# Ends of attention per 128 tokens with one inverse root on VectorE, earlier first gates and spread conditioning in a two-layer PEER block

## The chip, the cores and the metric

The kernel runs on one core of a Trainium2 chip. The metric is the device time of one execution in microseconds (us). The runs of the kernel before took 2294.64, 2292.17 and 2294.27 us, a median of 2294.27. One more execution was taken under the hardware profiler; every row below comes from it.

## The reference

A sequence of 256 tokens, 1024 wide, passes two layers and then two recurrent mixers (an LRU and a gated delta net) that are conditioned on a vector. One layer is, cut to what matters here:

```python
xn = rmsnorm(x, norm_mix[l])
u_pool, u_conv, u_diff, u_sc, u_mem = split(xn @ w_in[l])      # 256, 512, 768, 768, 256 columns
y_diff = diff_attention(u_diff)        # per head: softmax(q1 k1) - lam * softmax(q2 k2), times v
#   o = rmsnorm(o, subln_g) * (1 - lam_init)   per token and head (64 columns)
y_mem = memory_attention(u_mem, mem)   # softmax(q k) v over 256 memory rows, 4 heads
cat = stack([y_pool, y_conv, y_diff, y_sc, y_mem])             # groups 0 to 4, 256 columns each
cat = rmsnorm(cat, group_norm[l])      # per token and group
x = x + cat @ w_out[l]                 # 1280 x 1024
x = x + peer_ffn(rmsnorm(x, norm_ffn[l]))
```

The PEER part picks 16 of 16384 experts for each of 8 heads and token, with gates g. The kernel computes it densely: act = gelu(xn @ u.T) for all 16384 experts, times a gate matrix that is zero nearly everywhere, and that times v.

## The kernel before

All matrix products are in fp32 by three products of split operands: a tile from memory (`raw`) gives a high part `wh` (ScalarE, line 293) and a low part `wl` (VectorE, line 296), and TensorE adds high by high, high by low and low by high. TensorE is in use nearly throughout, so what counts is where it waits.

The program is a row of stages: mix0, peer0, mix1, peer1, lru, gdn, final. In the profiled execution mix0 ends at about 174 us, the u pass of peer0 runs to 630 and its v pass to 987, mix1 lasts to 1157, the u pass of peer1 to 1613 and its v pass to 1984.

**Mixing** (`mixing`, line 1033). The product with `w_in` runs in pieces; between its matmuls `tick` (here `fill`) advances background generators by a credit, and the order in which they are advanced is the order of the instructions on every engine. The generators are: a convolution (group 1), two lanes of differential attention (`diff_lane`, four units of two heads and 128 tokens each) and their end (`diff_end`), two lanes of memory attention (`mem_lane`) with `mem_end`, the short convolution (group 3) and the pooling (group 0). They take PSUM banks from a count (`bank`, `banks`, `free`) limited to `BANKS = 5`, and to `WBANKS = 4` once `wide`, the product with `w_out`, begins, since its four accumulators take the other four. `wide` takes the groups in the order `ZORDER = (3, 1, 0, 4, 2)` and calls `tick` until the next group is in the set `ready`: 8 matmuls of 128x512 per group, part and pair, 120 in all.

A group's norm needs an inverse root. `rsq` (lines 569 to 588) computes it by an integer guess and three Newton steps in 13 small instructions on GpSimd (POOL), after one VectorE instruction (line 577). Groups 0, 1 and 3 use it on sums over channels (`fT0`, `fT1`, `fT3`; their result goes through TensorE as a diagonal matrix). `diff_end` waits for all four units, squares (line 968), sums per head (972), calls `rsq` (`dsr`), scales (975 to 979), and goes to `finish_tok` (720), which squares again, calls `rsq` again (`ft2`), scales (728), transposes to channel layout on TensorE (`ident,do`) and hands the result to `into_z` (706), which writes the split parts `zTh` and `zTl`. `mem_end` has the one `rsq` of `finish_tok` (`ft4`; `mo` is its tensor).

**PEER** (`experts`, line 1215, and `v_pass`, 1365). The u pass has 64 steps of two expert tiles. Every few matmuls `tick` advances the scoring, the `routing` and then `scatter`, which builds the gates of the first 128 tokens as one-hot products: `hots` (lines 1275 and 1276, VectorE), `sums` (TensorE, `o,o`), `into` (1292 and 1294, evacuation into `big`). The gates of the other 128 tokens lie in memory and come back by `dense_load` (`gate<-dense`), to be multiplied in by `part` (line 1363). After the 64 steps the u pass runs whatever is left of routing and scatter, multiplies in the first two gate tiles, and splits the first tile of the v pass into `lasth` and `lastl`. The v pass then takes 128 tiles; in layer 1 it also advances, once per tile, the conditioning of the recurrent mixers (`adas`: products with `ada_w_2` on VectorE into `adacc`, lines 1448 and 1450, and a sum over partitions on TensorE, `adacc,ones`).

DMAs from memory to on-chip tiles are issued by SyncE (SP) in program order; an issue that must wait for a free buffer holds those behind it. `raw` has three buffers.

Of the kernel before, what the change touches and what calls it, by code (L numbers as in the profile page):

```python
# [86 lines left out]
class K:  # L87
# [617 lines left out]

    def into_z(self, l, g, ps):

        gc = self.col("group_norm", l)[:, 2 * g:2 * g + 2]
        i = yield from self.slot(g)
        zh, zl = [t[:, i:i + 2, :] for t in self.zT]  # L710
        for j in range(2):
            self.nc.scalar.activation(zh[:, j, :], ps[:, j, :], AF.Copy, scale=gc[:, j:j + 1])
        yield
        for j in range(2):
            self.nc.vector.scalar_tensor_tensor(zl[:, j, :], ps[:, j, :], gc[:, j:j + 1], zh[:, j, :],
                                                op0=OP.mult, op1=OP.subtract)
        self.ready.add(g)
        yield 0.8

    def finish_tok(self, l, g, y):  # L720
        ss = self.sm.tile([128, 2], F32, name=f"ftq{g}")
        junk = self.wk.tile([128, 2, 256], F32, name=f"fsq{g}", bufs=1)
        for c in range(2):
            self.nc.scalar.activation(junk[:, c, :], y[:, c, :], AF.Square, accum_out=ss[:, c:c + 1])
        yield
        rs = yield from self.rsq(ss, 256, [128, 2], f"ft{g}")
        for c in range(2):
            self.nc.vector.tensor_scalar(y[:, c, :], y[:, c, :], rs[:, c:c + 1], None, op0=OP.mult)
        yield 0.5
        ps = yield from self.bank()  # L730
        p = ps.rearrange("p (j t) -> p j t", j=2)
        for j in range(2):
            for c in range(2):
                self.tr(p[:, j, c * 128:(c + 1) * 128], y[:, c, j * 128:(j + 1) * 128])
        yield
        yield from self.into_z(l, g, p)
        self.free()
# [160 lines left out]
    def attend(self, ps, a, v, h0, o, lane):  # L898

        n = a.shape[1]  # L900
        for h in range(n):
            for k in range(2):
                i = 2 * (h % 2) + k
                self.tr(ps[h // 2][:, i * 128:(i + 1) * 128], a[:, h, k * 128:(k + 1) * 128])
            if h % 2:
                yield
        yield
        aT = self.wk.tile([128, n, 2, 128], F32, name="aT" + lane, bufs=1)
        for m in range(n // 2):
# [12 lines left out]

    def diff_lane(self, units, lane, V):
# [5 lines left out]
        for c, h0 in units:  # L929
# [11 lines left out]
            for i in range(2):  # L941
                nc.vector.scalar_tensor_tensor(s[:, i], pv[i], scale,
                                               V["alibi"][:, c, h0 + i, None, :].to_broadcast([128, 2, T]),
                                               op0=OP.mult, op1=OP.add)
                yield 0.7
                nc.vector.tensor_reduce(t[:, i, 0:2], s[:, i], axis=AX.X, op=OP.max, negate=True)
                yield 0.6
                for j in range(2):
                    nc.scalar.activation(s[:, i, j, :], s[:, i, j, :], AF.Exp, bias=t[:, i, j:j + 1],
                                         accum_out=t[:, i, 2 + j:3 + j])  # L950
            yield
            for i in range(2):
# [5 lines left out]
                yield 0.8  # L958
            yield from self.attend(ps, s[:, :, 0, :], V["v"], h0, V["o"][:, c, :], lane)
            V["n"] += 2  # L960

    def diff_end(self, l, V):
        nc = self.nc
        while V["n"] < 8:
            yield
        sq = self.wk.tile([128, 2, 256], F32, name="fsq2", bufs=1)
        o = V["o"]
        nc.scalar.activation(sq, o, AF.Square)
        yield
        yield  # L970
        ss = self.sm.tile([128, 8], F32, name="dss")
        nc.vector.tensor_reduce(ss, sq.rearrange("p c (h d) -> p (c h) d", d=64), axis=AX.X, op=OP.add)
        yield 0.6
        rs = yield from self.rsq(ss, 64, [128, 8], "dsr")
        nc.vector.tensor_scalar(rs, rs, 1.0 - (0.8 - 0.6 * math.exp(-0.3 * l)), None, op0=OP.mult)
        ov = o.rearrange("p c (h d) -> p (c h) d", d=64)
        nc.vector.tensor_mul(ov, ov, rs[:, :, None].to_broadcast([128, 8, 64]))
        yield 0.6
        nc.vector.tensor_mul(ov, ov, V["sub"][:, None, :].to_broadcast([128, 8, 64]))
        yield 0.6  # L980
        yield from self.finish_tok(l, 2, o)

    def mem_lane(self, units, lane, V):
# [5 lines left out]
        for c in units:  # L989
# [22 lines left out]
            V["n"] += 4  # L1012

    def mem_end(self, l, V):
        nc = self.nc
        while V["n"] < 8:
            yield
        r = self.sm.tile([128, 8], F32, name="mr")
        nc.vector.reciprocal(r, V["sum"])
        yv = V["o"].rearrange("p c (h d) -> p (c h) d", d=64)  # L1020
        nc.vector.tensor_mul(yv, yv, r[:, :, None].to_broadcast([128, 8, 64]))
        yield 0.7
        yield from self.finish_tok(l, 4, V["o"])
# [13 lines left out]
    def mixing(self, l):  # L1037
# [11 lines left out]
        M, V = {"n": 0}, {"n": 0, "alibi": alibi}  # L1049
# [29 lines left out]
        with self.ordered(*MPIN):  # L1079
# [12 lines left out]
            self.spawn(self.diff_end(l, V))  # L1092
# [6 lines left out]
            self.spawn(self.mem_end(l, M))  # L1099
# [5 lines left out]
            self.spawn(self.pool_mixer(l, self.kept(self.gemm_tok(xT, w, 18), "pu"), bd, poolm))  # L1105
            self.limit = WBANKS
# [107 lines left out]
    def experts(self, l, xT, big, skT, sc0, sc1):  # L1214
# [142 lines left out]
        self.split(big[:, 0, :], *[t[:, 0, :] for t in self.last])  # L1357
# [7 lines left out]
    def v_pass(self, l, big):  # L1365
# [23 lines left out]
        for e in range(128):  # L1389
# [771 lines left out]
RAW = 3  # L2161
VPIN = ("DVE", "Activation", "Pool", "PE")
# [131 lines left out]
```

## Time and profile before

| what | value |
|---|---|
| median of three runs | 2294.27 us (2292.17 to 2294.64) |
| the profiled execution, and its span | 2297.74 us, 2296.0 us |
| mean granted clock of TensorE over the span | 0.979 |
| TensorE (PE) busy | 2204.5 us, 96% |
| VectorE (DVE), ScalarE (ACT), GpSimd (POOL) busy | 1768.8, 1225.2 and 651.3 us |

The profiled execution took 1.74 us more than its span and 3.5 us more than the median. TensorE is busy for all but about 91 us of the span. [...]

### The profile page before, as it was taken

The page shows a single profiled execution, that of the slowest core. Times are in us where ns is not written, and L with a number is a line of the kernel's source. Part 1 is how long each engine was busy: PE and PEld are TensorE (multiplying, and loading weights), DVE is VectorE, ACT ScalarE, POOL GpSimd, SP SyncE. Part 2 cuts the span into 40 slices and gives each one's busy share as a digit, 9 for nine tenths or more (in the row PEclk, how much of TensorE's full clock was granted, in tenths as well). Part 3 has the DMA queues.
Part 4 walks back from the last instruction along what each step waited for, and adds up shares of the span by engine and source line. Part 5 has one row for each costly group of instructions (what it writes and reads, how often), then busy time and mean ns, then how long its engine had stood idle before and what let it go on. Part 6 is the DMA issues. An engine that isn't in the chain of part 4 may idle for free. (4 is left out here: it accounts for less than half of the span.)

```text
span 2296.0 us, 41803 instructions
## 1 busy us (share of the span) xinstructions
PE 2204.5 (96%) x15562; PEld 1990.1 (87%) x15562; DVE 1768.8 (77%) x3980; ACT 1225.2 (53%) x1999; POOL 651.3 (28%) x782
## 2 busy tenths in 40 slices
PE   8989999999999999999799999999999999999997
PEld 7869999999978888887689999999777788788886
DVE  7858999887756666678479999787798866788755
ACT  5545666644445555555355666444444445586754
POOL 3223787860000000012327887700000000101332
PEclk9989999999999999999799999999999999999998
DMA  8636777765577777785267777754898877744322
GB/s 305 201 95 169 182 183 191 187 154 153 159 215 214 225 209 219 219 302 175 68 176 176 187 192 188 156 154 152 288 318 312 313 230 216 220 146 134 115 82 74
DMA packets 206390, 439.31 MB, mean 191 GB/s; under 512 B 53454, under 2 KB 107854, under 8 KB 206187
## 3 DMA queue, kind: packets, MB, share of 16 engines
q1 hardware_dynamic: 169322, 436.50, 60.7%
q0 software_dynamic: 36864, 0.15, 4.3%
q8 instruction: 122, 2.00, 0.4%
q14 instruction: 82, 0.66, 0.1%
HBM read 416.49 MB, written 20.08 MB: 190 GB/s over the span
## 5 line engine op out<-in xcount | busy, mean ns | idle before, releaser
L293 ACT ACTIVATE wh<-raw 128x1024 fp32r<-128x1024 f32 x671 | 710.6, 1059 | 844.2 <-PE ps L263 649.4
L296 DVE TENSOR_TENSOR wl<-raw,wh 128x1024 fp32r<-128x1024 f32 x676 | 824.7, 1221 | 353.3 <-ACT wh L293 304.7
L263 PE MATMUL ps<-xTh,wh 128*128 128x256 f32 x2784 | 691.0, 287 | 4.5 <-ACT wh L293 4.3
L263 PE MATMUL ps<-xTl,wh 128*128 128x256 f32 x2784 | 682.8, 284 | 0.0
L346 POOL DMA_INDIRECT dense<-val,at x256 | 479.7, 1874 | 231.4 <-ACT wh L293 105.6
L263 PEld LDWEIGHTS ps<-xTh,wh 128*128 128x128 f32 x2784 | 533.8, 193 | 9.1 <-ACT wh L293 5.5
L263 PEld LDWEIGHTS ps<-xTl,wh 128*128 128x128 f32 x2784 | 534.0, 193 | 0.8 <-issue 0.4
L263 PE MATMUL ps<-xTh,wl 128*128 128x256 f32 x2784 | 398.0, 285 | 3.8 <-DVE wl L296 3.7
L263 PEld LDWEIGHTS ps<-xTh,wl 128*128 128x128 f32 x2784 | 360.5, 192 | 7.9 <-DVE wl L296 5.7
L263 PE MATMUL ps<-wh,cl 128*128 128x512 f32 x1008 | 313.9, 392 | 0.6 <-DVE cl L296 0.5
L263 PE MATMUL ps<-wh,ch 128*128 128x512 f32 x1008 | 312.6, 391 | 0.0
L263 PE MATMUL ps<-wl,ch 128*128 128x512 f32 x1008 | 311.1, 390 | 0.0
L263 PEld LDWEIGHTS ps<-wh,ch 128*128 128x128 f32 x1008 | 187.9, 188 | 48.9 <-ACT wh L293 9.5
L263 PEld LDWEIGHTS ps<-wh,cl 128*128 128x128 f32 x1008 | 187.0, 188 | 46.1 <-DVE cl L296 8.5
L263 PEld LDWEIGHTS ps<-wl,ch 128*128 128x128 f32 x1008 | 189.2, 188 | 40.0
L1630 POOL MEMSET c<- 128x6 f32 x16 | 1.6, 106 | 574.6 <-issue 489.1
L296 DVE TENSOR_TENSOR cl<-big,ch 128x256 fp32r<-128x256 f32 x252 | 105.2, 417 | 0.0
L293 ACT ACTIVATE ch<-big 128x256 fp32r<-128x256 f32 x252 | 101.3, 402 | 0.2
L578 POOL TENSOR_SCALAR mpy<-mpm 128x1 int32<-128x1 int32 x4 | 0.9, 232 | 333.0 <-DVE mpm L577 333.0
L1276 DVE TENSOR_SCALAR o<-iota,i1T,gT 128x128 f32<-128x128 f32 x256 | 90.1, 352 | 0.0
L1317 ACT ACTIVATE big<-ps 128x512 f32<-128x512 f32 (+17 forms) x128 | 69.9, 546 | 12.9 <-PE ps L263 12.6
L1363 DVE TENSOR_TENSOR big<-big,gate 128x128 f32<-128x128 f32 x256 | 72.5, 284 | 3.2 <-DMA gate<-dense 3.2
(563 smaller groups left out, 2517.6 us busy)
## 6 DMA issues: line engine op xcount, KB each, us to landing
raw<-in_peer_u_dram SPq DMA_DIRECT2D x256, 512.0 KB
raw<-in_peer_v_dram SPq DMA_DIRECT2D x256, 512.0 KB
adaw<-in_ada_w_dram SPq DMA_DIRECT2D x48, 512.0 KB
raw<-in_w_in_dram SPq DMA_DIRECT2D x40, 512.0 KB
dense<-zero SPq DMA_DIRECT2D x32, 512.0 KB
raw<-in_peer_wq_dram SPq DMA_DIRECT2D x32, 512.0 KB
gate<-dense SPq DMA_DIRECT2D x128, 128.0 KB
raw<-in_gdn_in_dram SPq DMA_DIRECT2D x32, 512.0 KB
```

Of the source, the lines that this page charges most:

```text
L263: self.nc.tensor.matmul(out, lhsT, rhs, start=start, stop=stop, skip_group_check=skip)
L293: self.nc.scalar.activation(h, x, AF.Copy)
L296: getattr(self.nc, low).tensor_sub(l, x, h)
L346: ins = self.nc.gpsimd.indirect_dma_start(out=self.dense[l], out_offset=bass.IndirectOffsetOnAxis(at[:, k:k + 1], 0), in_=val[:, k:k + 1], ...
L578: v.tensor_scalar(y.bitcast(I32), m.bitcast(I32), -0.5, float(0x5f3759df), op0=OP.mult, op1=OP.add)
L1276: nc.vector.tensor_scalar(o1[:, q, :], self.iota, i1T[:, t], gT[:, t], op0=OP.is_equal, op1=OP.mult)
L1317: nc.scalar.activation(v[:, :, n:], ps[:, :, n:], AF.Gelu)
L1363: self.nc.vector.tensor_mul(v, v, self.gq.popleft())
L1630: nc.gpsimd.memset(p[:, :, 0:3], 0.0)
```

## The change

Five edits:

1. `diff_end` and `mem_end` become one generator for each half of 128 tokens, which waits for that half's attention alone. Each has one inverse root in place of two (differential) or one (memory): the sum for the group norm is worked out from the per-head sums, so that both roots of the differential end are taken together on 5 columns. The new `root` is on VectorE: 10 instructions on 5 columns or 1. `end_chunk` scales, transposes one half and writes its part of `zTh`, `zTl`. There are two ends of each kind, so four roots in place of three, and the group is ready when both halves are.
2. `diff_lane` gives its two score banks back as soon as the scores are read, and takes one bank for the product with the values later on.
3. Ahead of `wide`, the bank limit is raised to 8 and `tick` is called until group 3 is ready; only then the limit falls to 4.
4. The u pass runs what is left of routing and scatter at step e = 120 instead of behind the last step, loads gate tiles 0 and 2 there, and multiplies in the first gates and splits the first tile at e = 124.
5. In layer 1 the v pass advances the conditioning on three of four tiles instead of on each.

The diff, cut to its core:

```diff
+    def root(self, m, shape, name):
+        v = self.nc.vector
+        y, t = [self.sm.tile(shape, F32, name=name + k) for k in "yt"]
+        v.tensor_scalar(y.bitcast(I32), m.bitcast(I32), -0.5, float(0x5f3759df), op0=OP.mult, op1=OP.add)
+        v.tensor_mul(t, y, y)
+        yield 0.15
+        for i in range(3):
+            v.scalar_tensor_tensor(t, t, -0.5, m, op0=OP.mult, op1=OP.mult)
+            v.scalar_tensor_tensor(y, t, 1.5, y, op0=OP.add, op1=OP.mult)
+            yield 0.15
+            if i < 2:
+                v.tensor_mul(t, y, y)
+        return y
...
     def attend (its last lines)
-        out = ps[1 if n == 2 else 0]
+        out = ps[0]
...
-        self.free(2)
+        self.free(n // 2)
...
     def diff_lane (after the scores are read, and at its end)
+                self.free()
...
+            ps = yield from self.banks(1)
             yield from self.attend(ps, s[:, :, 0, :], V["v"], h0, V["o"][:, c, :], lane)
-            V["n"] += 2
-
-    def diff_end(self, l, V):
+            V["n", c] += 2
+
+    def diff_end(self, l, V, c):
         nc = self.nc
-        while V["n"] < 8:
+        while V["n", c] < 4:
             yield
...
+        m, r, j = [self.sm.tile([128, n], F32, name="de" + x) for n, x in ((5, "m"), (4, "r"), (4, "j"))]
+        nc.vector.tensor_scalar(m[:, 0:4], ss[:, 0, :], 1.0 / 64, EPS, op0=OP.mult, op1=OP.add)
+        nc.vector.reciprocal(r, m[:, 0:4])
+        nc.vector.scalar_tensor_tensor(j, r, k * k / 256, ss[:, 1, :], op0=OP.mult, op1=OP.mult, accum_out=m[:, 4:5])
+        nc.vector.tensor_scalar(m[:, 4:5], m[:, 4:5], EPS, None, op0=OP.add)
         yield 0.6
-        nc.vector.tensor_mul(ov, ov, V["sub"][:, None, :].to_broadcast([128, 8, 64]))
-        yield 0.6
-        yield from self.finish_tok(l, 2, o)
+        y = yield from self.root(m, [128, 5], "de")
+        nc.vector.tensor_scalar(r, y[:, 0:4], y[:, 4:5], k, op0=OP.mult, op1=OP.mult)
+        yield from self.end_chunk(l, 2, V, c, r)
...
     def mixing
             for i in range(2):
                 self.spawn(self.diff_lane(units[i::2], f"d{i}", V))
-            self.spawn(self.diff_end(l, V))
+            for i in range(2):
+                self.spawn(self.diff_end(l, V, i))
...
+            self.limit = 8
+            while ZORDER[0] not in self.ready:
+                self.tick()
             self.limit = WBANKS
...
     def experts
         for e in range(0, 128, 2):
+            if e == EARLY:
+                while rt or sct:
+                    self.step(rt)
+                    self.step(sct)
+                for n in (0, 2):
+                    self.dense_load(l, n)
+            if e == EARLY + 4:
+                self.part(big, 0)
+                self.part(big, 1)
+                self.dense_load(l, 4)
+                self.split(big[:, 0, :], *[t[:, 0, :] for t in self.last])
             ps = self.gemm_T(xT, f"peer_u{l}", e)
             evac.append((e, ps))
         self.tick = self.pump
-        for e in (0, 2):
-            self.dense_load(l, e)
-        while rt or sct:
-            self.step(rt)
-            self.step(sct)
-        self.part(big, 0)
-        self.part(big, 1)
-        self.dense_load(l, 4)
-        self.split(big[:, 0, :], *[t[:, 0, :] for t in self.last])
         act(*evac.popleft())
...
     def v_pass
-                if e % 2 or l:
+                if e % 2 or (l and e % 4):
                     self.pump()
...
+EARLY = 120
```

How this moves instructions, at three places. First TensorE in the mixing of layer 1, where the product with `w_out` (`wh,zTh`, `wh,zTl`, `wl,zTh`) begins; `Tdk,Tdq` are scores and `dv,aTd` the product with the values of the differential attention, `ident,do` the transposes of its end, `fT3y` the root of group 3. Before:

```order
L263 MATMUL ps<-dv,aTd_12398 128x64 x4
L272 MATMUL ps<-ident,dsd_12348 128x128 x2
L263 MATMUL ps<-dv,aTd_12400 128x64 x4
L263 MATMUL ps<-ca,pw 128x256 x4
L263 MATMUL ps<-ident,fT3y 128x128 x2
L263 MATMUL ps<-wh,zTh 128x512 x4
L263 MATMUL ps<-wh,zTl 128x512 x2
L263 MATMUL ps<-ones,fsq_12511 128x1 x4
```

And after:

```order
L263 MATMUL ps<-pd,bd 128x256 x2
L272 MATMUL ps<-ident,do 128x128 x2
L263 MATMUL ps<-ca,pw 128x256 x4
L263 MATMUL ps<-ident,fT3y 128x128 x2
L917 MATMUL ps<-Tdk,Tdq 128x256 x4
L263 MATMUL ps<-wh,zTh 128x512 x4
L263 MATMUL ps<-wh,zTl 128x512 x4
L272 MATMUL ps<-ident,dsd_12371 128x128 x4
L263 MATMUL ps<-wl,zTh 128x512 x2
```

Before, all scores and products of the differential attention stand ahead of `wide`, and its transposes (four, `ident,do`) stand 16 wide matmuls into it. After, the first half's transposes (two) stand ahead of `wide`, and the last unit of one lane has its scores right ahead of it and the rest inside it. In the mixing of layer 0 all units stand ahead of `wide` after the change, where before the last one stood inside; the second half's transposes stand 24 wide matmuls into it, where before all four stood 75 in.

Second SyncE's DMA issues at the end of the u pass of layer 0. Before:

```order
L324 DMA raw<-in_peer_u_dram 128x1024 x67
L324 DMA raw<-in_peer_v_dram 128x1024 x4
L361 DMA gate<-dense_100 128x2x128 x2
L681 DMA mem<-in_mem_dram 128x1024
L324 DMA raw<-in_peer_v_dram 128x1024
L361 DMA gate<-dense_100 128x2x128
```

And after:

```order
L324 DMA raw<-in_peer_u_dram 128x1024 x63
L361 DMA gate<-dense_100 128x2x128 x2
L324 DMA raw<-in_peer_u_dram 128x1024 x4
L361 DMA gate<-dense_100 128x2x128
L324 DMA raw<-in_peer_v_dram 128x1024 x4
```

The gate loads have moved ahead of the last four u tiles and the first four v tiles.

Third VectorE there: `big<-ps,big` is `into`, `wl` the splits of the u and v tiles, `big<-big,ge` the activation's second half, `big<-big,gate` is `part`. Before, from the last of the `into` on:

```order
L1294 TENSOR_TENSOR big<-ps,big 128x122x4 x2
L296 TENSOR_TENSOR wl<-raw,wh 128x1024 x2
L1321 TENSOR_TENSOR big<-big,ge 128x2x128
...
L296 TENSOR_TENSOR wl<-raw,wh 128x1024 x2
L1363 TENSOR_TENSOR big<-big,gate 128x128 x2
L296 TENSOR_TENSOR lastl<-big,lasth 128x256
```

And after:

```order
L1329 TENSOR_TENSOR big<-ps,big 128x118x4 x2
L296 TENSOR_TENSOR wl<-raw,wh 128x1024
L1356 TENSOR_TENSOR big<-big,ge 128x2x128
L296 TENSOR_TENSOR wl<-raw,wh 128x1024 x2
L1356 TENSOR_TENSOR big<-big,ge 128x2x128
L296 TENSOR_TENSOR wl<-raw,wh 128x1024
L1400 TENSOR_TENSOR big<-big,gate 128x128 x2
L296 TENSOR_TENSOR lastl<-big,lasth 128x256
```

The last two `into` were for 122 columns of tiles and are for 118; ahead of them two groups of one-hots (8 instructions of line 1275 and 8 of 1276) stand with no `wl` between them, where before a `wl` stood between. The first `part` and `lastl` now have five `wl` between them and the v pass's next split.

## Rows read from the trace of the kernel before

**Rows 1.** The page: busy time, share of the span and instructions of each engine.

```profile
PE 2204.5 (96%) x15562; PEld 1990.1 (87%) x15562; DVE 1768.8 (77%) x3980; ACT 1225.2 (53%) x1999; POOL 651.3 (28%) x782
```

**Rows 2.** TensorE's waits, whole span: waiter <- releaser: us, times, longest.

```profile
PE ps L263 <- ACT lasth L293: 7.6, 2, 4.1
...
PE ps L263 <- POOL fT0y L584: 4.1, 1, 4.1
...
PE ps L263 <- POOL fT1y L584: 3.6, 1, 3.6
```

**Rows 3.** Windows, end of mix0: length; busy (count) PE, PEld, DVE, ACT, POOL; clock.

```profile
106.00:118.00 12.00, 11.66 (x85) 8.73 (x83) 6.43 (x19) 5.25 (x10) 5.83 (x21) 1.00 0.29 89
118.00:134.00 16.00, 15.45 (x84) 11.75 (x82) 11.17 (x25) 10.79 (x30) 0.61 (x3) 1.00 0.20 66
134.00:146.00 12.00, 7.61 (x30) 6.64 (x31) 4.79 (x13) 3.21 (x6) 6.12 (x37) 0.57 0.00 1
146.00:160.00 14.00, 10.44 (x45) 8.08 (x43) 5.74 (x10) 5.04 (x8) 5.10 (x26) 0.98 0.37 113
160.00:167.00 7.00, 6.50 (x19) 5.31 (x20) 3.85 (x6) 1.89 (x3) 0.00 (x0) 0.56 0.60 162
167.00:175.00 8.00, 7.71 (x36) 5.93 (x34) 4.71 (x9) 5.01 (x10) 0.00 (x0) 1.00 0.79 252
```

**Rows 4.** Windows, end of mix1, the same columns.

```profile
1081.00:1097.00 16.00, 13.65 (x101) 10.66 (x99) 10.34 (x22) 10.60 (x35) 5.17 (x18) 1.00 0.21 66
1097.00:1117.00 20.00, 12.51 (x43) 10.12 (x44) 9.61 (x30) 8.03 (x18) 6.53 (x28) 0.57 0.00 1
1117.00:1135.00 18.00, 14.43 (x64) 12.05 (x64) 7.40 (x15) 4.78 (x7) 8.29 (x38) 0.81 0.13 33
1135.00:1157.00 22.00, 20.35 (x85) 15.47 (x83) 10.06 (x12) 9.59 (x15) 0.00 (x0) 1.00 0.70 236
```

**Rows 5.** Timeline from u pass to v pass of layer 0, PE, then VectorE: start, us.

```profile
634.21 1.22 PE L263 MATMUL ps<-wh,lasth 128*128 128x512 f32 x2 [4.11 <-ACT lasth L293]
...
633.42 0.49 DVE L1363 TENSOR_TENSOR big<-big,gate 128x128 f32<-128x128 f32 x2 [1.92 <-DMA gate<-dense]
```

**Rows 6.** Windows, the first 4 us of both v passes.

```profile
634.20:638.20 4.00, 3.99 (x11) 3.21 (x12) 1.38 (x4) 0.81 (x3) 0.00 (x0) 0.62 0.86 299
...
1616.30:1620.30 4.00, 4.00 (x11) 3.06 (x12) 1.36 (x4) 2.29 (x5) 0.00 (x0) 0.57 0.74 219
```

**Rows 7.** Timeline of POOL, the chain ft2, first and last of 13.

```profile
156.47 0.19 POOL L578 TENSOR_SCALAR ft2y<-ft2m 128x2 int32<-128x2 int32 x1 [4.00 <-DVE ft2m L577]
...
159.77 0.19 POOL L584 TENSOR_TENSOR ft2y<-ft2t,ft2y 128x2 f32<-128x2 f32 x1
```

**Rows 8.** Groups by line, VectorE, 1085 to 1157 us: two small instructions.

```profile
L975 DVE TENSOR_SCALAR dsry<-dsry 128x8 f32<-128x8 f32 x1 | 0.2, 172 | 3.2 <-POOL dsry L584 3.2
...
L478 DVE TENSOR_SCALAR abq<-abq 128x1 f32<-128x1 f32 x1 | 0.1, 147 | 0.0
```

**Rows 9.** Groups by line, PE, 590 to 630 us: the one-hot sums.

```profile
L263 PE MATMUL ps<-o,o 128*128 128x128 f32 x42 | 5.6, 274 | 0.0
```

**Rows 10.** Timeline of VectorE, one group of one-hots, first and last of eight.

```profile
603.35 0.28 DVE L1275 TENSOR_SCALAR o<-iota,i2T 128x128 f32<-128x128 f32 x1
...
604.91 0.34 DVE L1276 TENSOR_SCALAR o<-iota,i1T,gT 128x128 f32<-128x128 f32 x1
```

**Rows 11.** Windows in v pass 0 and v pass 1; the products into `adacc`.

```profile
660.00:700.00 40.00, 40.00 (x178) 33.11 (x177) 25.63 (x44) 21.73 (x34) 0.00 (x0) 1.00 0.72 217
...
1720.00:1760.00 40.00, 40.00 (x169) 30.26 (x168) 33.98 (x53) 19.00 (x28) 0.00 (x0) 1.00 0.93 328
...
L1450 DVE SCALAR_TENSOR_TENSOR adacc<-adaw,cact,adacc x42: 1273/1276/1280, 1628.8 to 1827.0; 128x1024 f32<-128x1024 f32 x42
```

**Rows 12.** Timeline of POOL and VectorE at 1121 us.

```profile
1121.82 1.11 POOL L582 TENSOR_TENSOR fT1t<-fT1t,fT1m 128x2 f32<-128x2 f32 x1
...
1121.65 1.22 DVE L296 TENSOR_TENSOR wl<-raw,wh 128x1024 fp32r<-128x1024 f32 x1 [0.41 <-issue]
```

**Rows 13.** Timeline: where `do` came, mix0 (PE) and mix1 (VectorE).

```profile
160.50 1.09 PE L272 MATMUL ps<-ident,do 128*128 128x128 f32 x4 [4.05 <-DVE do L728]
...
1120.50 0.62 DVE L728 TENSOR_SCALAR do<-do,ft2y 128x256 f32<-128x256 f32 x2 [3.12 <-POOL ft2y L584]
```

More of the change, by code (lines that the diff above doesn't have):

```diff
@@ L704, in mem_prep @@
         self.mready = True
[L706 to L737, printed above, removed]
     def spread_rms(self, sq, name):
@@ L958, in diff_lane @@
                 yield 0.8
+            ps = yield from self.banks(1)
             yield from self.attend(ps, s[:, :, 0, :], V["v"], h0, V["o"][:, c, :], lane)
-            V["n"] += 2
-    def diff_end(self, l, V):
+            V["n", c] += 2
+    def diff_end(self, l, V, c):
         nc = self.nc
-        while V["n"] < 8:
+        while V["n", c] < 4:
             yield
+        k = 1.0 - (0.8 - 0.6 * math.exp(-0.3 * l))
+        o = V["o"][:, c, :]
+        ov = o.rearrange("p (h d) -> p h d", d=64)
@@ L966, in diff_end @@
         sq = self.wk.tile([128, 2, 256], F32, name="fsq2", bufs=1)
-        o = V["o"]
-        nc.scalar.activation(sq, o, AF.Square)
+        nc.scalar.activation(sq[:, 0, :], o, AF.Square)
+        nc.vector.tensor_mul(ov, ov, V["sub"][:, None, :].to_broadcast([128, 4, 64]))
+        yield 0.35
+        nc.scalar.activation(sq[:, 1, :], o, AF.Square)
         yield
         yield
-        ss = self.sm.tile([128, 8], F32, name="dss")
-        nc.vector.tensor_reduce(ss, sq.rearrange("p c (h d) -> p (c h) d", d=64), axis=AX.X, op=OP.add)
+        ss = self.sm.tile([128, 2, 4], F32, name="dss")
@@ L973, in diff_end @@
+        nc.vector.tensor_reduce(ss.rearrange("p a h -> p (a h)"), sq.rearrange("p c (h d) -> p (c h) d", d=64), axis=AX.X,
+                                op=OP.add)
         yield 0.6
[L974 to L977, printed above, removed]
-        yield 0.6
@@ new lines, in diff_end, with end_chunk @@
+        nc.vector.tensor_scalar(m[:, 4:5], m[:, 4:5], EPS, None, op0=OP.add)
+        yield 0.6
+        y = yield from self.root(m, [128, 5], "de")
+        nc.vector.tensor_scalar(r, y[:, 0:4], y[:, 4:5], k, op0=OP.mult, op1=OP.mult)
+        yield from self.end_chunk(l, 2, V, c, r)
+    def end_chunk(self, l, g, V, c, r):
+        o, cs = V["o"][:, c, :], slice(c * 128, (c + 1) * 128)
+        ov = o.rearrange("p (h d) -> p h d", d=64)
+        self.nc.vector.tensor_mul(ov, ov, r[:, :, None].to_broadcast([128, 4, 64]))
+        yield 0.5
+        ps = yield from self.bank()
+        p = ps.rearrange("p (j t) -> p j t", j=2)
+        for j in range(2):
+            self.tr(p[:, j, cs], o[:, j * 128:(j + 1) * 128])
+        yield
+        gc = self.col("group_norm", l)[:, 2 * g:2 * g + 2]
+        i = yield from self.slot(g)
+        zh, zl = [t[:, i:i + 2, cs] for t in self.zT]
+        for j in range(2):
+            self.nc.scalar.activation(zh[:, j, :], p[:, j, cs], AF.Copy, scale=gc[:, j:j + 1])
+        yield
+        for j in range(2):
+            self.nc.vector.scalar_tensor_tensor(zl[:, j, :], p[:, j, cs], gc[:, j:j + 1], zh[:, j, :],
+                                                op0=OP.mult, op1=OP.subtract)
+        self.free()
+        V["z"].add(c)
+        if len(V["z"]) == 2:
+            self.ready.add(g)
+        yield 0.5
@@ L1011, in mem_lane, with mem_end @@
             yield from self.attend(ps, a, V["v"], 0, V["o"][:, c, :], lane)
-            V["n"] += 4
-    def mem_end(self, l, V):
+            V["n", c] += 4
+    def mem_end(self, l, V, c):
         nc = self.nc
-        while V["n"] < 8:
+        while V["n", c] < 4:
             yield
[L1018 to L1023, printed above, removed]
+        o = V["o"][:, c, :]
+        sq = self.wk.tile([128, 2, 256], F32, name="fsq4", bufs=1)[:, c, :]
+        nc.scalar.activation(sq, o, AF.Square)
+        r, q, m = [self.sm.tile([128, n], F32, name="me" + x) for n, x in ((4, "r"), (4, "q"), (1, "m"))]
+        nc.vector.reciprocal(r, V["sum"][:, 4 * c:4 * c + 4])
+        nc.vector.tensor_mul(q, r, r)
+        yield 0.3
+        yield
+        ss = self.sm.tile([128, 4], F32, name="mes")
+        nc.vector.tensor_reduce(ss, sq.rearrange("p (h d) -> p h d", d=64), axis=AX.X, op=OP.add)
+        nc.vector.scalar_tensor_tensor(q, q, 1.0 / 256, ss, op0=OP.mult, op1=OP.mult, accum_out=m)
+        nc.vector.tensor_scalar(m, m, EPS, None, op0=OP.add)
+        yield 0.6
+        y = yield from self.root(m, [128, 1], "me")
+        nc.vector.tensor_scalar(r, r, y, None, op0=OP.mult)
+        yield from self.end_chunk(l, 4, V, c, r)
     def normed(self, V, key, y, nh, hd, col, name):
@@ L1048, in mixing @@
         mq, dq, mn, dn = self.col("mem_qk_norm", l), self.col("diff_qk_norm", l), (4, 64), (8, 32)
-        M, V = {"n": 0}, {"n": 0, "alibi": alibi}
+        M, V = [{("n", 0): 0, ("n", 1): 0, "z": set()} for _ in range(2)]
+        V["alibi"] = alibi
         mk = []
@@ L1098, in mixing @@
                 self.spawn(self.mem_lane([i], f"m{i}", M))
-            self.spawn(self.mem_end(l, M))
+            for i in range(2):
+                self.spawn(self.mem_end(l, M, i))
             poolm = self.xp.tile([128, 2, D], F32, name="xs").rearrange("p c (g t) -> p c g t", g=4)
```

## The prediction, made before the changed kernel ran

> **What bounds the kernel now.** I read the page first: TensorE is busy 2204.5 of 2296.0 us [rows 1], so only some 91 us are idle in all, and a change in other engines' work can win no more than the part of these that it touches, plus what the clock loses behind them. Then TensorE's waits [rows 2]: those that the changed lines answer for are named there, `lasth` (7.6 us in two), `fT0y` (4.1) and `fT1y` (3.6). Then windows and timelines at these places.
>
> End of mix0 [rows 3]: between 118 and 167 us TensorE idles 0.55 + 4.39 + 3.56 + 0.50 = 9.0 us, the last long gap for `do` [rows 13]. Behind each long gap the clock falls: 0.57 over 7.61 busy us and 0.56 over 6.50 cost 3.3 + 2.9 = 6.2 us (busy time times the share of the clock that is missing). In all 15.2 us lie between this stretch and an unbroken one.
>
> End of mix1 [rows 4]: idle 2.35 + 7.49 + 3.57 + 1.65 = 15.1 us; clock 12.51 x 0.43 + 14.43 x 0.19 = 8.1 us. In all 23.2 us.
>
> From u pass to v pass [rows 5]: TensorE starts the v pass 4.11 us after the last product of the u pass, released by `lasth`, and that by `part`, whose VectorE instruction waited for the gate's DMA, issued only behind the first v tiles. Then 11 matmuls pass in 4 us at a clock of 0.62 [rows 6], where 18 do at full clock (36 in 8 us, last window of [rows 3]): 7 x 0.222 = 1.6 us. Layer 1 shows the same, 3.5 us (the other part of the 7.6 [rows 2]) and again 11 matmuls, at 0.57 [rows 6]. Together 10.8 us.
>
> **The change part by part.**
>
> *Ends of attention (edits 1 to 3).* Removed: three chains of 13 POOL instructions per mixing. One takes 3.5 us, 156.47 to 159.96, 0.27 us a step [rows 7]; with `dsr` and `ft2` in sequence the differential end spent 7 us in them. Added: four roots of 10 VectorE instructions and some 25 more small ones around them, about 65 per mixing. VectorE instructions of 1 to 8 columns take 0.147 to 0.172 us [rows 8], so one root is 1.6 us when nothing stands between, and all 65 are 10.4 us. VectorE was busy 6.4 + 11.2 of the 28 us before 134 in mix0 [rows 3], and 10.3 + 9.6 of 36 in mix1 [rows 4]: there is room, but not beside the second half's attention without delay.
>
> [...]
>
> What decides is where `wide` begins and whether it then runs unbroken. Its 120 matmuls at 0.222 us are 26.7 us. In mix0, following the new order of the instructions with the old durations, both halves' attention and the product of group 3 are through at about 122 us, and `wide` begins at an estimated 125.5 (near 118 before). Then 26.7; about 18 small matmuls inside at 0.14 (85 in 11.7 us [rows 3]), 2.5; a stall of about 4 for the roots of groups 0 and 1, which stay on POOL; 3 at half clock behind the gap ahead of `wide`. The end is then at about 162, where it was about 174. I take 10 us, not 12, since a walk by hand leaves out queues. Bounds: 15.2 (nothing idle), and 4 (one wait of the two goes, as the one on `do` [rows 13]).
>
> In mix1 the means of group 3 stood on VectorE behind `mo`, which waited for `ft4`. By the new order they come some 11 us earlier, and `wide` begins at an estimated 1097 (near 1117 before). Then 26.7; 34 small matmuls, 4.8; 3 for the stall at `fT1y`, which remains (its sums stand eight wide matmuls ahead of it, and POOL's chain takes 3.5); 3 at half clock; 1.5 for a late tile of `w_out`: 1136, where it was 1157. I take 18 of the 21; bounds 23.2 and 7 (3.6 for `fT1y` [rows 2] and 3.1 for `do` [rows 13], the clock as it was).
>
> *First gates (edit 4).* Nothing then stands between the last u product and the first v product, and the 10.8 us go. The gate loads are issued ahead of the last four u tiles, which wait behind them; they read memory that was filled long before. The price is the drain at e = 120. Two groups of one-hots stand on VectorE without a `wl` between them, 1.9 us each (603.35 to 605.25 [rows 10]), and TensorE's sums for both stand ahead of the next u product. So it waits for the second group, some 2.4 us with the queue, of which sums that were due anyway fill a part (eight matmuls, 1.1 us, by 42 in 5.6 [rows 9]). I take 1.5 per layer, from 0 (under the last product) to 4 (both groups bare). Net 10.8 - 3.0 = 7.8; bounds 10.8 and 2.8.
>
> *Conditioning (edit 5).* A window of 40 us holds 169 matmuls in v pass 1 and 178 in v pass 0 [rows 11], 2 us less work. Most of that is the sums over partitions, which stay. VectorE is busy 34 of 40 us there, 26 in v pass 0 [rows 11]; with a product into `adacc` in each tile, 1.28 us, it lags a little, and one tile in four without it lets it catch up. Over the 198 us of these products (1628.8 to 1827.0 [rows 11]) the 2 us per window would be 10, of which I take 1.5, bounds 0 and 3.6 (a third). Its cover is the rest of the v pass: at three quarters of the pace it ends near 1628.8 + 198.2 x 4/3 = 1893, and the pass ends at 1984.
>
> **Sum.** 10 + 18 + 7.8 + 1.5 = 37.3 us of 2297.7 in the profiled execution, 2260.4. That execution lay 3.5 us above the median of the runs, so I forecast 2257.
>
> **The rivals.**
>
> *A. The ends on VectorE come late.* The 65 small instructions stand in one queue with the means of groups 0 and 1 and with the `wl` of `w_out`, and VectorE becomes what TensorE waits for. If three quarters of the 10.4 us lie on the path in each mixing, 16 us are lost: a gain of 21.3, 2273. For it: the second half's root stands ahead of `fT1m` in the queue. Against: the steps of a root are interleaved with other work, and VectorE is half idle there [rows 3, 4].
>
> *B. The passage gives nothing.* The drain costs what the 10.8 us gave: a gain of 29.5, 2265. For it: both groups stand bare. Against: it takes 5.4 us per layer, more than the two groups together.
>
> *C. POOL slows.* At 1121.82 a POOL instruction took 1.11 us in place of 0.19, for as long as VectorE's two-operand `wl` lasted [rows 12]. With 65 more VectorE instructions the chains left, `fT3`, `fT0` and `fT1`, on which `wide` waits, are caught more often: 0.9 us per catch, some three more per mixing, 5.5 us: a gain of 32, 2262. [...]
>
> *D. Attention moves from inside `wide` to ahead of it (slower).* `wide` now waits for group 3, and group 3's product stands behind attention in the queues. If attention is no faster than before, `wide` in mix0 begins when `do` came, 160.5 [rows 13]; with 26.7 + 2.5 + 3 it ends at 192.7, over 18 later. In mix1 it begins at 1120.5 [rows 13] and ends about where it did. With 9.3 gained elsewhere that is 9 slower, 2303. In mix0 any begin past 142 loses. For it: in mix0 the new order does put all score units ahead of `wide`. Against: the banks that the fourth unit waited for come back early.
>
> *E. The mixings don't change.* Attention itself is late, not its end: only 9.3 are gained, 2285. Against: the gaps are named for roots and their scaling [rows 2, 13].
>
> **How the numbers follow.** The forecast has 0.55, A 0.17, B 0.10, C 0.08, D 0.05, E 0.05. For eight in ten I go from 2244 (all parts at their upper bounds, 52.8 us, would be 2241) to 2280, which holds A, B and C; D and E stay out. What a measurement of this kernel can tell from no change is about 0.2%, 4.6 us: faster 0.91; same 0.04, between D and E; slower 0.05, from D.
>
> **What would show it.** In the new profile: no wait on `lasth`, clock 1.00 in the first 4 us of both v passes, and a wait of about 2 us near e = 120; `wide` beginning near 125 and 1097 and lasting some 36 and 39 us, no wait on `do`, one on `fT1y` left; 171 or more matmuls per 40 us in v pass 1. I am wrong if TensorE's waits name `dey`, `mey` or a `wl` for more than 5 us in a mixing (A), if POOL's chains there take over 4.5 us each (C), or if `wide` of mix0 begins past 142 (D).

## The result, and the profile after

The changed kernel takes 2263.13 us (median of four runs, 2258.99 to 2265.53), the kernel before 2293.22 beside it: a ratio of 0.9868, 95% interval 0.9853 to 0.9884, some 30 us less. I had forecast 2257 with a range from 2244 to 2280. The profiled execution took 2263.26 us, its span is 2261.4, 34.6 us less than the span before.

The page after, busy time by engine:

```profile
PE 2190.3 (97%) x15562; PEld 1982.9 (88%) x15562; DVE 1779.3 (79%) x4110; ACT 1225.1 (54%) x2001; POOL 639.3 (28%) x704
```

TensorE does the same 15562 matmuls and is busy 14 us less than in [rows 1]: part of the gain is not idle time but matmuls that no longer run at half clock (the mean granted clock is 0.986, before 0.979). Half clock is a granted share of 0.50 of the full one, 1.00: in the changed kernel five matmuls of 128x512 take 2.30 us from 139.46 on, where the window below shows 0.50, and four take 0.94 from 147.61 on, at 1.00; a value between the two is the mean of a stretch with both. VectorE has 130 instructions more and is busy 10.5 us longer over both layers, POOL has 78 fewer.

TensorE's waits after, whole span:

```profile
PE ps L263 <- POOL fT0y L584: 3.9, 1, 3.9
PE ps L263 <- ACT zTh L293: 3.7, 4, 1.4
PE ps L263 <- POOL fT1y L584: 3.0, 1, 3.0
...
PE ps L263 <- DVE o L1311: 1.3, 2, 0.6
```

Against [rows 2]: `lasth` is gone, and so is `do` in mix0 ([rows 13]; 0.4 us of it are left in mix1). The two POOL roots are still there, now `fT1y` in mix0 and `fT0y` in mix1. The wait on `o` is new: the drain at e = 120.

Windows after, end of mix0, then end of mix1 (columns as in [rows 3]):

```profile
107.00:125.00 18.00, 17.01 (x134) 15.13 (x133) 16.28 (x68) 14.67 (x42) 7.95 (x27) 1.00 0.11 30
125.00:131.00 6.00, 5.61 (x31) 4.80 (x31) 5.24 (x40) 1.39 (x2) 4.77 (x16) 1.00 0.02 5
131.00:136.00 5.00, 2.04 (x10) 1.43 (x9) 3.18 (x6) 1.58 (x2) 3.67 (x11) 0.86 0.51 145
136.00:142.00 6.00, 4.59 (x16) 3.71 (x16) 3.21 (x9) 2.17 (x7) 0.00 (x0) 0.50 0.26 85
142.00:165.00 23.00, 22.72 (x92) 17.88 (x92) 10.49 (x13) 10.31 (x15) 0.00 (x0) 0.94 0.64 197
...
1087.00:1097.00 10.00, 9.47 (x56) 8.19 (x57) 8.10 (x40) 5.09 (x12) 4.24 (x15) 1.00 0.15 52
1097.00:1102.00 5.00, 1.07 (x7) 0.84 (x6) 2.34 (x4) 0.62 (x2) 3.40 (x11) 0.86 0.29 72
1102.00:1108.00 6.00, 5.45 (x18) 4.23 (x18) 3.51 (x9) 1.79 (x5) 0.00 (x0) 0.55 0.07 29
```

The stretch ahead of `wide` (which begins at 125.39) is now full: 17 of 18 us busy at clock 1.00, with VectorE busy 16.3. One long gap per mixing is left, and behind it the clock is at half, in mix0 0.50 from 136 to 142, in mix1 0.55 from 1102 to 1108.

The passage from u pass to v pass in layer 0 (timeline of TensorE), and below it the first 4 us of both v passes as windows:

```profile
621.81 0.64 PE L263 MATMUL ps<-xTh,wl 128*128 128x256 f32 x4
622.28 0.62 PE L263 MATMUL ps<-wh,lasth 128*128 128x512 f32 x2
```

```profile
622.30:626.30 4.00, 4.00 (x20) 3.23 (x19) 2.49 (x5) 2.51 (x6) 0.00 (x0) 1.00 0.83 250
...
1587.40:1591.40 4.00, 4.00 (x20) 3.24 (x19) 2.51 (x5) 2.62 (x7) 0.00 (x0) 1.00 0.67 211
```

No gap, full clock, 20 matmuls in both where [rows 6] have 11.

By places in TensorE's timeline (the first transposes of `big`, the first product with `lasth`, the first transposes of `xs` in mix1, the last product with `lasth`), the time between each pair before, and by how many us each profile differs from it:

| stretch | before, us | changed | ends only | gates only | conditioning only | before again |
|---|---|---|---|---|---|---|
| mix0 | 174.56 | -9.64 | -10.44 | -0.52 | -0.48 | +1.42 |
| u pass 0 | 459.65 | -2.29 | -0.31 | -2.76 | +0.12 | -0.35 |
| v pass 0 | 358.89 | -1.53 | -1.36 | -1.45 | +1.57 | +0.15 |
| mix1 | 164.15 | -13.33 | -12.44 | -4.45 | -4.96 | -0.32 |
| u pass 1 | 459.05 | -2.15 | -0.05 | -2.15 | -0.06 | +0.36 |
| v pass 1 | 368.03 | -3.80 | +2.30 | -0.66 | -2.25 | +0.33 |
| the rest | 311.67 | -1.86 | -0.10 | +0.99 | -4.24 | -3.79 |

The last four columns are experiments, below. The last one is the same program once more: a stretch can differ by 4 us with nothing changed.

### The profile page after: what moved, and what is told of

Its sections match the earlier page's. It is cut to its first block, busy times and chain, and to the rows that moved or that the text cites. A ratio compares the mean times of both kernels' runs of the same rounds, so it can differ in the third digit from the quotient of the medians.

```text
span 2261.4 us, 41814 instructions
## 1 busy us (share of the span) xinstructions
PE 2190.3 (97%) x15562; PEld 1982.9 (88%) x15562; DVE 1779.3 (79%) x4110; ACT 1225.1 (54%) x2001; POOL 639.3 (28%) x704
## 5 line engine op out<-in xcount | busy, mean ns | idle before, releaser
L263 PEld LDWEIGHTS ps<-wh,ch 128*128 128x128 f32 x1008 | 188.0, 188 | 48.8 <-ACT wh L293 10.4
L1352 ACT ACTIVATE big<-ps 128x512 f32<-128x512 f32 (+15 forms) x128 | 69.8, 546 | 11.3 <-PE ps L263 11.0
L1310 DVE TENSOR_SCALAR o<-iota,i2T 128x128 f32<-128x128 f32 x256 | 75.6, 296 | 0.0
```

The lines of the kernel that those rows point to most:

```text
L263: self.nc.tensor.matmul(out, lhsT, rhs, start=start, stop=stop, skip_group_check=skip)
L1310: nc.vector.tensor_scalar(o2[:, q, :], self.iota, i2T[:, t], None, op0=OP.is_equal)
L1352: nc.scalar.activation(v[:, :, n:], ps[:, :, n:], AF.Gelu)
```

## The experiments

**Each part alone.** Ends only is the changed kernel with `experts` and the conditioning of before; the other two are one edit each in the kernel before:

```diff
-                if e % 2 or l:
+                if e % 2 or (l and e % 4):
```

> The kernel before with edits 1 to 3 (ends of attention, banks, wait for group 3) alone. Theory: the stages are additive, and this part gives what the profile after shows in the two mixings, 9.6 us in mix0 and 13.3 in mix1, so about 23 us of gain, 2270 by the median; the waits on lasth stay (7.6 us). Rival: part of the mixing gain in the profile after comes from a different state of clock and queues that the other edits left behind; then the gain is under 18 us.

> The kernel before with edit 4 (routing ended at e = 120, first gates at 124) alone. Theory: per layer 2.2 us less up to the first v product (5.7 of wait and half clock less 1.6 for the drain, less another 1.8 that the profile after lost at the head of the u pass only in layer 0) and 1.6 us of half clock less behind it: 7 to 8 us in all, 2286. Rival: the drain costs what the passage gives, no change (2293).

> The kernel before with edit 5 (conditioning on three of four tiles in layer 1) alone. Theory: v pass 1 gets 2 us shorter (VectorE catches up on every fourth tile), 2291. Rival one: nothing, since the sums over partitions are what costs (2293). Rival two: it also accounts for the 1.9 us that the stages behind the v pass became shorter in the profile after, and gives 4 us (2289).

Measured: ends only 2275.13, ratio 0.9928 (0.9914 to 0.9942), 16.5 us of gain; gates only 0.998 (0.9972 to 0.9989), 4.6 us; conditioning only 0.9987 (0.9977 to 0.9997), 3 us. The sum of the three is 24, the whole 30; with half-widths of 3.2, 2.0 and 2.3 beside the whole's 3.6 (5.7 as the root of their squares) the gap of 6 is at the edge of what they allow, so whether the parts add up stays open. (Between the medians the three are 17.6, 6.1 and 4.0 us, together 27.7.) The table agrees for the mixings (ends only: 10.4 and 12.4 us) and for the gates (2.8, 1.5, 2.2 and 0.7 us in the four stretches that they touch). For the ends its run gave less than the 23 expected and less than the rival's bound of 18, though the stretches of its own profile show the mixing gain in full. What differs is v pass 1, 2.3 us longer there, and the profile of before that the table starts from, 5.0 us above the median of the executions beside this run.

Unlooked for: gates only and conditioning only each show mix1 4.5 to 5 us shorter, with mixing code that is the same. So the kernel before was profiled again.

> The kernel before, unchanged, profiled once more. Theory: in the profile of before mix1 took 4.5 to 5 us more than in the two runs that share its mixing code (gates alone 159.7, conditioning alone 159.2, before 164.2 from the mixing's first transposes to its last product), since TensorE waited 3.6 us there for fT1y at a clock that had come back, and paid with half clock again; that is chance of one execution, so this one shows 158 to 161 and no wait of over 1 us on fT1y. Rival: edits 4 and 5 each shorten mix1 by something that they leave behind, and this one shows 164.

It shows 163.83 us in mix1, as the first profile: the theory's number did not come, the rival's did. What the profiles do show is the clock. Kernel before again, then gates only, the windows ahead of `wide` in mix1:

```profile
1098.00:1118.00 20.00, 12.24 (x42) 9.88 (x42) 9.69 (x30) 7.98 (x18) 6.22 (x27) 0.57 0.00 1
1118.00:1136.00 18.00, 14.33 (x63) 12.09 (x64) 7.72 (x15) 4.46 (x8) 8.60 (x39) 0.81 0.09 29
```

```profile
1092.00:1110.00 18.00, 10.51 (x42) 8.48 (x42) 9.40 (x29) 7.87 (x18) 6.10 (x27) 0.72 0.00 1
1110.00:1128.00 18.00, 17.78 (x70) 15.15 (x71) 8.64 (x16) 5.22 (x8) 8.77 (x39) 0.72 0.14 43
```

Before, the clock falls early, the 42 small matmuls take longer (12.24 us there, 10.51 with the gates alone), it comes back at about 1118, and TensorE then waits 3.58 us for `fT1y` and pays with half clock again. With the gates alone it falls later, TensorE is still slow when `fT1y` is due, and has no wait there. Whether that is chance or something the other edits shift stays open; two profiles of each kind don't decide it. The run times lean to chance. Gates and conditioning alone gained 6.1 and 4.0 us between the medians, where the stretches that they touch account for 7.0 and 2.3; another 4.5 to 5 us in mix1 hardly fits beside these. And the 46 executions of the kernel before that stand beside the experiments run from 2287.42 to 2298.83 us: six at a mean granted clock of 0.984 take 2288.7 on average, four at 0.978 take 2295.8, so half-clock stretches come and go within one program. Both profiles of it, at 2297.74 and 2295.61, lie above the medians. If a mix1 of some 159.5 us is the usual one, the ends gain 8 to 9 us there and not 12 to 13, and ends only comes to some 18 us, as its runs say; no run shows this directly.

**The parts of the ends.** Roots on POOL: the root's body as in `rsq`, on `nc.gpsimd`. No wait:

```diff
-            self.limit = 8
-            while ZORDER[0] not in self.ready:
-                self.tick()
             self.limit = WBANKS
```

Banks kept:

```diff
     def attend
-        out = ps[0]
+        out = ps[1 if n == 2 else 0]
...
-        self.free(n // 2)
+        self.free(2)
     def diff_lane
-                self.free()
...
-            ps = yield from self.banks(1)
```

Wait with 5 banks leaves out the line `self.limit = 8` alone.

> The changed kernel with the four roots of the ends on POOL again (the same 13 small instructions as before, one end per 128 tokens as after). It parts the engine of the root from the cutting into halves. Theory: the gain of the mixings comes from the halves and the banks, and the engine matters little, since three quarters of the roots' time lies beside other work: mix0 and mix1 within 2 us each of the changed kernel, 2263 to 2267. Rival: the engine matters, POOL has the chains of groups 0, 1 and 3 in the same queue, and these come 3 us or more later in each mixing: 2269 or more.

> The changed kernel without the bank limit of 8 and without the wait for group 3 ahead of wide (two statements of edit 3). Theory: wide then takes its four banks while scores and products are still under way, the last ones are spread over it, and it has the unbroken run no longer: 3 to 6 us lost in the two mixings, 2266 to 2269. Rival (my rival D turned round): the wait only moves attention ahead of wide, and without it wide begins earlier by what it then loses: 2263 within 2 us.

> The changed kernel with the score banks kept to the end of a unit (edit 2 undone). Theory: what let the second half's attention come forward is the banks, so with them kept wide begins later (mix0 past 130, mix1 past 1092) and 5 to 9 us of the mixings' gain go: 2268 to 2272. Rival: the halves alone do it, since each end waits for two units only: 2263 within 2 us.

> The changed kernel with the wait for group 3 kept but the bank limit left at 5 during it (in place of 8). It parts the two halves of edit 3, whose removal cost 21 us. Theory: with five banks the lanes stand in line for a bank while TensorE has little else to do, the gaps drop the clock to half as they did without the wait, so most of it comes back: mix0 ends past 175, 2275 or more. Rival: the wait itself is what counts (four banks are not taken by wide while attention needs them), and five banks do: 2263 to 2267.

| us against the profile of the changed kernel | `wide` of mix0 begins | mix0 | mix1 | median, ratio to before |
|---|---|---|---|---|
| changed | 125.39 | 0 | 0 | 2263.13, 0.9868 |
| roots on POOL | 127.45 | +8.30 | +5.49 | 2276.34, 0.9929 (0.9913 to 0.9945) |
| no wait | 146.96 | +19.87 | +5.11 | 2284.77, 0.9961 (0.9946 to 0.9976) |
| wait with 5 banks | 143.35 | +14.11 | +7.48 | 2283.85, 0.9963 (0.9950 to 0.9977) |
| banks kept | 132.11 | +12.02 | -0.41 | 2276.49, 0.9932 (0.9917 to 0.9948) |

Each of the four costs 13 us or more. Taking back the root's engine, edit 3 and edit 2 one by one loses 48 us in sum, more than the whole gain, so the parts lean on one another. (The profiled execution with the roots on POOL lay 5 us above its median.) For the roots on POOL the rival was right: the engine matters as much as giving the banks back early. For the lines of edit 3 theory and rival were both far too small: without them 21.6 of the 30 us are lost. The wait alone gives nothing back, since with five banks as much is lost (there the theory was right): it is the limit of 8 during the wait that counts. The kept banks cost more than expected in mix0 and nothing in mix1. In the last three rows mix0 is slower than in the kernel before, by 10.2, 4.5 and 2.4 us (9.64 taken from 19.87, 14.11 and 12.02). No run takes back the halves or the single root of edit 1, so what these give by themselves is not shown.

Where 20 us go is in the windows of mix0 without the wait:

```profile
107.00:118.00 11.00, 8.29 (x48) 7.05 (x47) 9.31 (x37) 9.07 (x29) 0.00 (x0) 0.74 0.16 49
118.00:125.00 7.00, 7.00 (x32) 5.74 (x30) 4.30 (x15) 2.13 (x5) 3.42 (x13) 0.50 0.00 0
125.00:135.00 10.00, 10.00 (x46) 6.70 (x45) 2.74 (x15) 2.10 (x4) 0.00 (x0) 0.61 0.17 52
135.00:145.00 10.00, 7.34 (x32) 5.85 (x31) 6.36 (x35) 4.36 (x12) 3.32 (x13) 0.73 0.01 2
145.00:155.00 10.00, 8.37 (x29) 7.11 (x29) 4.32 (x18) 2.15 (x4) 2.77 (x16) 0.50 0.01 2
```

TensorE idles 2.7 us between 107 and 113, and is then busy without a break until 137, yet at half clock until 132 (1.00 from 133). Busy time times the missing share of the clock is 2.2 + 3.5 + 3.9 + 2.0 + 4.2 = 15.8 us over these five windows; the changed kernel, whose clock is 1.00 up to 131, loses 0.3 + 2.3 + 1.4 = 4.0 in all of its own. So by this estimate some 12 of the 20 us are clock.

**What is left.** The remaining waits name POOL. Its chain for `fT1` in mix0 of the changed kernel, four of its 13 instructions:

```profile
129.26 0.45 POOL L578 TENSOR_SCALAR fT1y<-fT1m 128x2 int32<-128x2 int32 x1
129.79 1.05 POOL L579 TENSOR_TENSOR fT1t<-fT1y 128x2 f32<-128x2 f32 x1
...
132.85 1.22 POOL L584 TENSOR_TENSOR fT1y<-fT1t,fT1y 128x2 f32<-128x2 f32 x1
...
135.30 0.19 POOL L584 TENSOR_TENSOR fT1y<-fT1t,fT1y 128x2 f32<-128x2 f32 x1
```

It takes 6.2 us where the chain of [rows 7] took 3.5. That one was the shortest of the twelve chains of before, though: those of groups 0, 1 and 3, which stay on POOL, took 3.7 to 5.6 us before the change and take 4.1 to 6.2 after it. The two long ones fall on two splits `wl` of VectorE (129.57 to 130.79 and 132.78 to 134.01), as in [rows 12]. In the next runs `spread_rms` takes its root from VectorE: for groups 0, 1 and 3, for 0 and 1, or for all three in layer 1 alone. The last two kernels also have scatter paced (advanced on every tick from expert tile 64 on), which is also tried by itself:

```diff
     def spread_rms
-        rs = yield from self.rsq(ps[:, 0:2], 256, [128, 2], name)
+        m = self.sm.tile([128, 2], F32, name=name + "m")
+        self.nc.vector.tensor_scalar(m, ps[:, 0:2], 1.0 / 256, EPS, op0=OP.mult, op1=OP.add)
+        rs = yield from self.root(m, [128, 2], name)
     def tick (experts)
-                if state["tick"] % 3:
+                if state["tick"] % 3 or state["tile"] >= 64:
```

> The changed kernel with the roots of groups 0, 1 and 3 too on VectorE (root in place of rsq in spread_rms). Theory: POOL's chains, stretched to 4.4 to 6.2 us by VectorE's two-operand instructions, are what wide still waits for (fT1y 3.0 us, fT0y 3.9 us, and half clock behind each); on VectorE a root takes 2 to 3 us, the two waits shrink below 1.5 us each and the clock stays up: 6 to 9 us of gain on 2263, about 2255. Rival: VectorE is the busy engine there (5.2 of 6 us at 125 to 131), its queue delays the roots as much as POOL did: within 2 us of 2263.

> The changed kernel with scatter advanced on every tick from expert tile 64 on (in place of two ticks of three), so that nothing is left to drain at e = 120. Theory: the drain costs 1.6 us per layer (7.0 us between two products of the u pass where 2.9 and three sums of 0.84 are due), so 3 us are gained, 2260, and the wait on the one-hots (o, 1.3 us in two) goes. Rival: the denser one-hots make VectorE late for the wl of the u tiles elsewhere, and nothing is gained: 2263.

> The changed kernel with scatter paced as in the run before and the roots of groups 0 and 1 alone on VectorE (group 3's stays on POOL). Theory: wide then begins as early as in the changed kernel (125 to 128), since the convolution's chain on VectorE is not held up by a root ahead of wide, and the waits on fT0y and fT1y shrink: mix0 1 to 3 us shorter than the changed kernel, mix1 3 to 5, u passes 1.5 each: 2254 to 2257. Rival: the order on VectorE decides, mix0 loses what mix1 gains: 2259 or more.

> The changed kernel with scatter paced and all three group roots on VectorE in layer 1 only. Theory: the stages are additive: mix1 4.5 us shorter, as with the roots on VectorE in both layers, mix0 as in the changed kernel, u passes 1.5 each shorter: 2255. Rival: 2258 or more, if mix1's gain there came with mix0's delay.

| us against the profile of the changed kernel | mix0 | u pass 0 | mix1 | u pass 1 | median, ratio to before |
|---|---|---|---|---|---|
| roots of 0, 1, 3 on VectorE | +1.67 | -0.23 | -4.47 | 0.00 | 2260.93, 0.9870 (0.9855 to 0.9884) |
| scatter paced | +2.20 | -1.53 | +0.88 | -1.50 | 2261.86, 0.9862 (0.9843 to 0.9882) |
| roots of 0, 1, paced | -4.76 | -1.98 | -5.52 | -1.08 | 2250.30, 0.9821 (0.9802 to 0.9839) |
| roots of layer 1, paced | +0.42 | -1.97 | -2.60 | -1.50 | 2258.94, 0.9854 (0.9834 to 0.9874) |

Pacing takes the drain away, 1.5 us per u pass, as expected; over the whole run that is less than the runs scatter. With all three roots on VectorE theory and rival are both half right: mix1 gains, but in mix0 the convolution's chain (`ca`) comes 2.09 us late behind a root, and `wide` begins 3.7 us later. With group 3 left on POOL both mixings gain 5 us, more than expected, and the kernel, at 2250.3, is the best of all here, 0.9821 of the kernel before. With all three in layer 1 alone mix1 gains 2.6 us and not the 4.5 expected, and the time is the rival's: the stages do not simply add. Its windows of mix0:

```profile
125.00:131.00 6.00, 5.16 (x28) 4.35 (x28) 5.23 (x46) 2.01 (x3) 0.00 (x0) 1.00 0.02 5
131.00:136.00 5.00, 3.42 (x20) 2.50 (x19) 5.00 (x26) 2.72 (x6) 0.00 (x0) 1.00 0.31 105
136.00:142.00 6.00, 5.11 (x23) 4.16 (x24) 4.13 (x11) 2.32 (x4) 0.00 (x0) 1.00 0.67 219
142.00:160.20 18.20, 17.92 (x78) 14.11 (x77) 9.22 (x12) 9.25 (x14) 0.00 (x0) 1.00 0.70 217
```

There are still gaps (its longest wait is 2.20 us, for `do`), but behind none of them did the clock fall: 1.00 throughout, in mix1 too. That fits gains of 4.8 and 5.5 us where the two waits were 3.0 and 3.9 us long.

## Why the prediction was right, point by point

**Ends, mix0: 10 predicted, 9.6 measured.** `wide` begins at 125.39, forecast 125.5; it lasts 39.3 us, forecast 36.2. The waits in it are 4.4 us (forecast 4; 2.96 of them for `fT1y`) and the half clock costs 4.0 (3). The matmuls themselves take 30.9 (29.2): 22 small ones stand inside, not 18, and a wide one at full clock takes 0.234 us (four in 0.94). My 0.222 came from 36 matmuls in 8 us [rows 3], of which four are the small transposes of `big`. So the walk was 3 us short, and the 2 us that I took off it for queues nearly made up for that: that 10 and 9.6 lie so close is in part luck.

**Ends, mix1: 18 predicted, 13.3 measured; the mis-sized term.** Counted from the start of the mixing, `wide` begins 3.9 us later than walked: 1.6 of it are there at the last product with `w_in`, and `wide` follows that by 17.6 us where I had 15.3. It then lasts 42.7 us, forecast 39.0. Together 7.6 of the 21 us walked are missing. The roots are not what was too small: waits inside `wide` are 5.0 us (3.93 of them for `fT0y`), where I had 3 and 1.5 for a late tile that did not come late, and half clock costs 2.6, where I had 3. The matmuls take 35.2 and not 31.5: 54 small ones stand inside `wide` and not 34 (among them 16 products `dv,aTd` and 8 transposes `dsd` of the attention), and the wide ones again take 0.234. A before that was long by 4.5 us does not explain the miss; it would leave the ends an even smaller gain here.

**First gates: 7.8 predicted; measured 2.3 + 2.2 in the u passes and 1.5 in v pass 0**, with the like in v pass 1 some 7.5. With the gates alone v pass 1 gave 0.7 and the four stretches 7.0, and the runs say less: 4.6 us by the ratio, with an interval of 2.5 to 6.4. Before, in layer 0, SyncE issued the two gate loads at 629.27, behind four v tiles whose issues took 8.97 us from 620.01 on; in the changed kernel it issues them at 594.35. The drain was walked through rightly. Its three sums and wait, TensorE's timeline in the changed kernel:

```profile
594.14 1.12 PE L263 MATMUL ps<-xTh,wl 128*128 128x256 f32 x8
595.10 1.95 PE L263 MATMUL ps<-o,o 128*128 128x128 f32 x16
597.67 1.75 PE L263 MATMUL ps<-o,o 128*128 128x128 f32 x8 [0.63 <-DVE o L1311]
...
601.17 1.12 PE L263 MATMUL ps<-xTh,wl 128*128 128x256 f32 x8
```

7.03 us from `wl` to `wl` where 2.88 is the usual step and the sums of three groups are due 2.5: 1.6 us, forecast 1.5. The half clock behind the old gap was not certain: with the ends only, the gap is 3.34 us in layer 0 and 3.45 in layer 1, and the 4 us behind it are at 1.00 in the one and at 0.50 in the other:

```profile
623.50:627.50 4.00, 4.00 (x17) 3.19 (x18) 1.59 (x5) 2.11 (x5) 0.00 (x0) 1.00 0.90 336
...
1591.70:1595.70 4.00, 4.00 (x9) 3.14 (x10) 1.36 (x4) 2.29 (x5) 0.00 (x0) 0.50 0.80 245
```

**Conditioning: 1.5 predicted; 2.25 in v pass 1 by itself**, 3 us by the runs with an interval of 0.7 to 5.3. A 40-us window holds 171 or 172 matmuls (1675 to 1755), as forecast.

**The sum.** 37.3 predicted, 34.6 between the spans, 30 between the medians. The profile of before that I started from lay 4.5 us above the later median, the one after did not; and 1.9 us of the 34.6 lie in stages that nothing touched, which differ by 3.8 between two profiles of the same kernel.

**The rivals.** The measured time lies nearer to C's 2262 than to my 2257, but by the lengths of the chains C accounts for little of the difference. My sign for it, chains over 4.5 us, was given by three of the six chains that stay on POOL before the change already (5.6, 5.4 and 4.7), and by four of six after it (6.2, 5.1, 4.8 and 4.8); in mix1 the three grew by 0.1 to 1.1 us. What C starts from is there again: POOL instructions of 1.05 and 1.22 us, where the shortest of that chain take 0.19, end 0.05 and 0.06 us behind a `wl` of 1.22; why they end together no run shows. Moving the roots of groups 0 and 1 to VectorE gave back some 5 us per mixing, but that is whole chains, waits and clock together, not the stretch alone.

D did not come. Its mechanism is seen where edit 3 is taken apart: `wide` of mix0 begins at 143.35 and 146.96, and mix0 is slower than before. Its bound of 142 was too high: with the banks kept `wide` begins at 132.11 and mix0 is still 2.4 us slower than before, since `wide` lasts 44.6 us there and not the 32 that the bound was made of. B and E did not come either: gates and mixings both gained. Nor did A: no wait in either mixing names `dey`, `mey` or a `wl`. One reason, which I had not seen, is in the last section.

## What to carry to other kernels

Count a gap on TensorE at its length plus the half-clock stretch behind it where the trace shows one (in mix0 0.50 from 136 to 142 behind the wait of 2.96 us, and none behind one of 2.20 with the roots of groups 0 and 1 on VectorE), and look for the few missing buffers (here three PSUM banks during 20 us) that string small gaps together: 21 us here, where the engine of four roots was worth 13. When work is moved between VectorE and POOL, look at what the move does to the chains that stay on POOL (here 3.7 to 5.6 us before, 4.1 to 6.2 after). And profile the kernel before more than once, and hold its stretches against the run times: a stretch that is read as recoverable may be one execution's, and here two profiles agreed where the run times lean to a shorter one.

## What was not expected of the hardware

Small VectorE instructions of independent chains overlap in this trace, with starts 0.075 us apart. In the changed kernel, timeline of VectorE where three roots are interleaved:

```profile
125.97 0.15 DVE L602 TENSOR_TENSOR met<-mey 128x1 f32<-128x1 f32 x1
126.04 0.17 DVE L594 TENSOR_SCALAR dey<-dem 128x5 int32<-128x5 int32 x1
126.12 0.22 DVE L598 SCALAR_TENSOR_TENSOR met<-met,mem 128x1 f32<-128x1 f32 x2
...
127.40 0.15 DVE L599 SCALAR_TENSOR_TENSOR dey<-det,dey 128x5 f32<-128x5 f32 x1
127.47 0.15 DVE L598 SCALAR_TENSOR_TENSOR met<-met,mem 128x1 f32<-128x1 f32 x1
```

Twenty-one start from 125.97 to 127.47, one each 0.075 us, though most last 0.15. By that step the 65 of a mixing are an estimated 5 us and not the 10.4 that rival A and the cost in my working were built on; a lone chain steps by 0.19 us (without the wait: 128.73, 128.92, 129.11), against POOL's 0.27 [rows 7]. Instructions on five columns are recorded with 0.15 to 0.17 us, those on one column with 0.15; but the price measured was 0.19 us from step to step of one chain and 0.075 with several chains side by side, half of the 0.15 that most are recorded with and that I had added up.
